# A five-stage transformer kernel on one core: a fixed order of two engines at the stages' ends, and later places for two pieces of the fourth stage

## The chip, the cores and the metric

The kernel runs on one core of a Trainium2 chip. The metric is the device time of one execution in microseconds (us), as the median of several runs. Engines are called as the profile calls them: PE (TensorE, matrix products), DVE (VectorE), ACT (ScalarE), POOL (GpSimd), SP (SyncE, which here only issues DMAs).

## The reference, cut to what matters

Two blocks run one after the other on a sequence of 256 tokens of width 1024. The first is two layers of a hybrid mixer, the second a feed-forward part, an attention and gating part ("mix") and another feed-forward part. Every part normalises its input, multiplies it by large weight matrices and adds the result to the running activations:

```python
def hybrid_layer(x, norm_g, w_in, ..., w_out, rel_bias):
    u = split_columns(rmsnorm(x, norm_g) @ w_in)
    ...
    return x + jnp.concatenate([y_ml, y_gla, y_dsa], axis=-1) @ w_out

def second_block(x, ...):
    h = h + 0.5 * swiglu(rmsnorm_2(h, ffn1_norm[l]), ffn1_w_gate[l], ffn1_w_up[l], ffn1_w_down[l])
    n = rmsnorm_2(h, mix_norm[l])
    z = n @ w_in[l]
    ...
    gm = chunked_spatial_gating(zg[..., :G_WIDTH], zg[..., G_WIDTH:], ...)
    gates = jax.nn.sigmoid(n @ w_gate[l] + b_gate[l])
    merged = gates[..., :D] * (attn @ w_branch_attn[l]) + gates[..., D:] * (gm @ w_branch_gmlp[l])
    h = h + merged @ w_out[l]
    h = h + 0.5 * swiglu(rmsnorm_2(h, ffn2_norm[l]), ffn2_w_gate[l], ffn2_w_up[l], ffn2_w_down[l])
    return rmsnorm_2(h, final_norm)
```

The spatial gating multiplies a lower-triangular 128x128 matrix per channel group (`gmlp_w_s`) with the layer-normalised half of z.

## The kernel before

**Stages.** `run` goes through five stages: layer0, layer1, ffn1, mix, ffn2. The running activations `x` stay on the chip as 2 tiles of 128 tokens (t = 0, 1) by 1024 columns.

**Weights.** All weights come as 362 units of 128x1024 floats. `weights` fetches one: a DMA into `raw` (3 buffers), a copy on ACT that rounds it to `hi` (L113), a subtraction on DVE that leaves the rest in `lo` (L114); 5 pairs of `hi` and `lo` exist, so the pair of a unit is free for the unit five later as soon as PE has used it. Each product is made of three matmuls (`mm3`): high by high, high by low, low by high. Activations are split in the same way by `split` (ACT L139 for the high part, DVE L140 for the low part).

**A stage's end.** `out_proj` adds the stage's product to `x`. Its last four units are computed by token tile: for t = 0 and then t = 1, for each half h of the columns, for each of the last two units. After each (t, h) `residual` adds the PSUM result to `x` on DVE (L320, L322 where it is scaled). Once both halves of a token tile are in `x`, `normed` prepares the next stage's input: two squares with row sums on ACT (L308), their sum `r` on DVE (L310), a power on POOL (L311), two products on DVE that write `xs` (L314). `turn` then transposes `xs` on PE in eight 128x128 pieces (`xT`, L223), and `split` makes the high and low parts of the next stage's input of them. The transposes of tile 0 are issued inside the last product of the old stage (t = 1, h = 1, after the first of the two units), those of tile 1 inside the first projection of the next stage (`proj_a`, after three of its four units for tile 0).

**The order of the work.** Instructions are issued in program order with priorities: `high_priority(self.ahead(LEAD))` moves weight fetches up to 500 places forward, normalisation and splits up to 1000. Where an instruction stands in its engine's queue follows from these priorities in a scheduler. Each engine then runs its queue in order. `order(ins)` adds edges that fix the order of the given instructions on one engine without a semaphore.

**Side jobs.** `start` puts a generator on a list, `tick` advances each by one `yield`; the large projections tick after each unit, so that attention and gating pieces are strewn between them. In mix, `attention` computes logits (`al`, L963), a softmax on DVE and ACT (last step L596), waits three ticks, transposes the probabilities on PE (`apT`, L223) and, after both tiles of a head group, multiplies them with the values (`aO`, L981). `spatial` loads the triangular matrices (`wsT`, L1000, 512 KB), clears their upper halves on POOL in eight instructions (L1002), normalises the two tiles of `vg` on DVE (with two small POOL steps `lnr`, L215 and L216, between), and then issues its matmuls (`sgp`, L1025) in two groups of eight. The projection that runs around them is `gatep`, 16 units of 16 matmuls (L200, L201).

Of the kernel before, what the change touches and what calls it, by code (L numbers as in the profile page):

```python
# [34 lines left out]
class Net:  # L35
    def __init__(self, ctx, tc, a, out, dbg=None):
# [18 lines left out]
        self.jobs, self.ready = [], []  # L55
# [46 lines left out]
    def weights(self):  # L102

        nc = self.nc
        if self.ready:
            return self.ready.pop()
        with self.tc.high_priority(self.ahead(LEAD)):
# [5 lines left out]
            nc.scalar.copy(hi, raw)  # L113
            nc.vector.tensor_sub(lo, raw, hi.bitcast(F32))  # L114
        return hi, lo
# [16 lines left out]
    def order(self, ins):  # L132

        for a, b in zip(ins, ins[1:]):
            self.tc.add_manual_dep(b.ins, a.ins.name, NOSYNC, reason="order")

    def split(self, hi, lo, src):

        self.nc.scalar.copy(hi, src)  # L139
        self.nc.vector.tensor_sub(lo, src, hi.bitcast(F32))  # L140
# [8 lines left out]
    def proj_a(self, x, name, by_token=None):  # L149
# [13 lines left out]
        for t in range(2):  # L163
            for u in range(4):
                self.rows(ps, x, 2 * u, u == 0, u == 3, (t,), ws[u])
                if t == 0 and u == 2:
                    self.turn()
# [109 lines left out]
    def norm(self, g_src):  # L277
# [6 lines left out]
        def fill(t):  # L284
            with self.tc.high_priority(self.ahead(2 * LEAD)):
                halves = self.normed(t, g)

            def turn():
                for b, xs in enumerate(halves):
                    ps = self.transposes([xs[:, P * k:P * (k + 1)] for k in range(4)], "xT")  # L290
                    ks, ts = slice(4 * b, 4 * b + 4), slice(P * t, P * (t + 1))
                    with self.tc.high_priority(self.ahead(2 * LEAD)):
                        self.split(xh[:, ks, ts], xl[:, ks, ts], ps)
# [8 lines left out]
    def normed(self, t, g):  # L302
# [4 lines left out]
        for h in range(2):  # L307
            nc.scalar.activation(xs[h], self.x[:, t, 512 * h:512 * (h + 1)], AF.Square, scale=1.0 / 32, accum_out=ss[:, h:h + 1])  # L308
        r = self.small([P, 1], "r")
        nc.vector.scalar_tensor_tensor(r, ss[:, 0:1], EPS, ss[:, 1:2], ALU.add, ALU.add)  # L310
        nc.gpsimd.tensor_tensor(r, r, self.mhalf[:, 0:1], ALU.pow)  # L311
        for h in range(2):
            sl = slice(512 * h, 512 * (h + 1))
            nc.vector.scalar_tensor_tensor(xs[h], self.x[:, t, sl], r, g[:, sl], ALU.mult, ALU.mult)  # L314
        return xs

    def residual(self, t, half, ps, scale=None):
        sl = self.x[:, t, 512 * half:512 * (half + 1)]
        if scale is None:
            self.nc.vector.tensor_add(sl, ps, sl)  # L320
        else:
            self.nc.vector.scalar_tensor_tensor(sl, ps, scale, sl, ALU.mult, ALU.add)  # L322

    def out_proj(self, y, nk, scale=None, need=0):
# [622 lines left out]
    def attention(self, qk, vs, y):  # L947
# [4 lines left out]
        for hg in range(2):  # L952

            pT = self.work([P, 4, 384], "pT2", 2)
            for t in range(2):
# [11 lines left out]
                yield  # L967
                yield
                yield
# [25 lines left out]
    def spatial(self, v, ug, y):  # L995
# [12 lines left out]
        for t in range(2):  # L1008
# [9 lines left out]
            yield  # L1018
        for u in range(2):
# [15 lines left out]
    def run(self, stages):  # L1035
# [16 lines left out]
        for pool, part in (("hybrid", ("layer0", "layer1")), ("ffn1", ("ffn1",)), ("mix", ("mix",)), ("ffn2", ("ffn2",))):  # L1052
# [158 lines left out]
```

## Time and profile before

| what | value |
|---|---|
| device time, median of 3 runs | 1138.05 us (1137.65 to 1139.64) |
| the profiled execution's own time | 1138.0 us |
| its span | 1136.3 us |
| PE busy | 1119.2 us, 98% of the span |
| DVE, ACT, POOL busy | 813.2 us (72%), 616.6 us (54%), 93.6 us (8%) |
| chain that ended last, by engine | PE 90%, DVE 6%, ACT 2%, DMA 1% |
| granted TensorE clock | 9 tenths or more in all 40 slices |

The span is the time from the first to the last instruction of the program; the device time holds another 1.7 us around it. A busy PE says only that matmuls overlap without a hole in the record: matmuls of 512 columns take 0.39 us each in the record but start every 0.23 us. So lost time is read from the starts of neighbouring matmuls.

### The profile page before, as it was taken

The numbers are of one execution on the slowest core, as the hardware profiler recorded it, in microseconds if no ns is written. First come the engines' busy times: TensorE is split into PE (matmuls) and PEld (weight loads), VectorE is DVE, ScalarE is ACT, GpSimd is POOL, SyncE is SP. The second block draws the span as 40 slices with busy tenths as digits, with TensorE's granted clock in tenths as the row PEclk, the third lists the DMA queues.
The fourth block names the chain that finished last, engine by engine and source line by source line (L and its number), as shares of the span: only waits on it lengthen the run. The fifth ranks groups of instructions, "written<-read, shape, count | busy, mean of one in ns | idle before, by whom it ended". The sixth has DMA issues, their size and how long they took to land.

```text
span 1136.3 us, 16695 instructions
## 1 busy us (share of the span) xinstructions
PE 1119.2 (98%) x6330; PEld 962.0 (85%) x6330; DVE 813.2 (72%) x1236; ACT 616.6 (54%) x950; POOL 93.6 (8%) x133
## 2 busy tenths in 40 slices
PE   8999999999999999999999999999999999999997
PEld 5888889898798888989878888887887997888886
DVE  5697897886668879778756777646597577777743
ACT  5645755554465576456445555434566545555532
POOL 1111101121011210112100000000001000000000
PEclk9999999999999999999999999999999999999999
DMA  8846545556564654456557565666654565666662
GB/s 274 262 146 205 185 136 158 161 170 189 163 200 146 198 167 143 136 155 180 173 159 225 183 189 187 199 190 198 218 168 131 174 190 177 197 189 188 195 192 75
DMA packets 59465, 203.75 MB, mean 179 GB/s; under 512 B 6700, under 2 KB 9652, under 8 KB 59384
## 3 DMA queue, kind: packets, MB, share of 16 engines
q1 hardware_dynamic: 59384, 202.68, 57.2%
q8 instruction: 50, 0.82, 0.3%
q14 instruction: 31, 0.25, 0.1%
HBM read 201.46 MB, written 2.11 MB: 179 GB/s over the span
## 4 chain that ended last, share of the span: by engine, by line
PE 90%; DVE 6%; ACT 2%; DMA 1%; issue 1%; POOL 0%; SPq 0%; DVEq 0%; POOLq 0%; ACTq 0%
PE op L147 19%; PE fg L200 6%; PE fu L200 6%; PE mq L147 4%; PE mk L147 4%; PE mo L147 4%; PE mz L147 4%; PE mv L147 3%; PE fg L201 3%; PE fu L201 3%; DVE lo L114 2%; PE gatep L200 2%; PE brp L147 2%; PE dz L147 2%; PE iq L147 2%; PE dk L147 2%
## 5 line engine op out<-in xcount | busy, mean ns | idle before, releaser
L114 DVE TENSOR_TENSOR lo<-raw,hi 128x1024 fp32r<-128x1024 f32 x362 | 446.6, 1236 | 223.5 <-ACT hi L113 222.2
L113 ACT CAST hi<-raw 128x1024 fp32r<-128x1024 f32 x362 | 378.7, 1048 | 374.6 <-PE op L147 89.2
L200 PE MATMUL fu<-x,hi 128*128 128x512 f32 x288 | 101.0, 395 | 0.0
L200 PE MATMUL fg<-x,hi 128*128 128x512 f32 x288 | 100.9, 394 | 0.0
L201 PE MATMUL fg<-x,lo 128*128 128x256 f32 x288 | 80.1, 278 | 0.0
L201 PE MATMUL fu<-x,lo 128*128 128x256 f32 x288 | 80.0, 278 | 0.0
L147 PE MATMUL op<-hi,hh 128*128 128x512 f32 x176 | 68.7, 390 | 0.0
L147 PE MATMUL op<-lo,hh 128*128 128x512 f32 x176 | 68.6, 390 | 0.0
L147 PE MATMUL op<-hi,hl 128*128 128x512 f32 x176 | 68.6, 390 | 0.0
L200 PEld LDWEIGHTS fg<-x,hi 128*128 128x128 f32 x288 | 54.1, 188 | 12.6
L200 PEld LDWEIGHTS fu<-x,hi 128*128 128x128 f32 x288 | 54.1, 188 | 12.5
L201 PEld LDWEIGHTS fg<-x,lo 128*128 128x128 f32 x288 | 54.2, 188 | 0.1
L201 PEld LDWEIGHTS fu<-x,lo 128*128 128x128 f32 x288 | 54.2, 188 | 0.0
L311 POOL TENSOR_TENSOR r<-r,mhalf 128x1 f32<-128x1 f32 x12 | 6.6, 554 | 541.7 <-DVE r L310 541.7
L147 PE MATMUL op<-hi,yh 128*128 128x512 f32 x128 | 51.2, 400 | 0.0
L147 PE MATMUL op<-lo,yh 128*128 128x512 f32 x128 | 50.0, 391 | 0.0
L147 PE MATMUL op<-hi,yl 128*128 128x512 f32 x128 | 49.9, 390 | 0.0
L147 PE MATMUL mq<-x,hi 128*128 128x256 f32 x256 | 48.2, 289 | 0.0
L147 PE MATMUL mk<-x,hi 128*128 128x256 f32 x256 | 46.8, 285 | 0.0
L200 PE MATMUL gatep<-x,hi 128*128 128x512 f32 x128 | 46.2, 404 | 0.0
L660 DVE SCALAR_TENSOR_TENSOR cacc<-pad,cols,cacc 128x256 f32<-128x256 f32 x96 | 41.0, 479 | 0.0
L147 PE MATMUL mv<-hi,x 128*128 128x512 f32 x128 | 40.8, 400 | 0.0
(360 smaller groups left out, 2588.6 us busy)
## 6 DMA issues: line engine op xcount, KB each, us to landing
raw<-in_w SPq DMA_DIRECT2D x362, 512.0 KB, 3.5
x<-in_x SPq DMA_DIRECT2D x2, 512.0 KB, 5.1
g_bc<-in_norm_g SPq DMA_DIRECT2D x2, 512.0 KB, 4.3
mlg<-in_ml_norm_g SPq DMA_DIRECT2D x2, 512.0 KB, 5.4
skew<-strips SPq DMA_DIRECT2D x4, 256.0 KB, 5.3
pen<-skew SPq DMA_DIRECT2D x8, 128.0 KB, 2.9
mb<-M SPq DMA_DIRECT2D x2, 512.0 KB, 4.3
g_bc<-in_ffn_norm SPq DMA_DIRECT2D x2, 512.0 KB
```

Source lines behind the costliest of these rows:

```text
L113: nc.scalar.copy(hi, raw)
L114: nc.vector.tensor_sub(lo, raw, hi.bitcast(F32))
L147: self.nc.tensor.matmul(out, lhsT=lhsT, rhs=rhs, start=first and i == 0, stop=last and i == 2)
L200: nc.tensor.matmul(ps, lhsT=wh[:, ks], rhs=self.x2[:, k], start=k == 0, stop=False)
L201: nc.tensor.matmul(ps[:, 1, :], lhsT=wl[:, ks], rhs=self.x2[:, k, 0, :], start=False, stop=k == KT - 1)
L311: nc.gpsimd.tensor_tensor(r, r, self.mhalf[:, 0:1], ALU.pow)
L660: nc.vector.scalar_tensor_tensor(acc[:, c, :], pad[:, c, 1 + i:1 + i + S], w(i), acc[:, c, :], ALU.mult, ALU.add)
```

## The change

At every stage's end but the last, `out_proj` now fetches the first four units of the next stage itself (`fetch`, called u0 to u3 below in their order of use) and gives ACT and DVE one fixed order for what belongs to the end: the four units' copies and subtractions, the squares, the products `xs`, the splits, the residuals. The residual of tile 1's first half stands behind the splits of tile 0. The subtraction of the third unit, u2, goes to POOL behind the power of tile 0, but not where the next stage is mix (`self.third`). The unit fetched after the last splits is ordered behind them (`self.pins`). In mix, `attention` waits four ticks before it transposes the probabilities where it waited three, and `spatial` waits two more ticks before its matmuls.

```diff
     def weights(self):
         nc = self.nc
         if self.ready:
-            return self.ready.pop()
+            return self.ready.pop(0)
+        return self.fetch()[0]
...
+    def fetch(self, pool=False):
+        nc = self.nc
         with self.tc.high_priority(self.ahead(LEAD)):
             raw = self.wr.tile([P, 1024], F32, tag="raw", name="raw")
             nc.sync.dma_start(raw, self.a["w"][self.unit])
             self.unit += 1
             hi = self.ws.tile([P, 1024], F32R, tag="hi", name="hi")
             lo = self.ws.tile([P, 1024], F32R, tag="lo", name="lo")
-            nc.scalar.copy(hi, raw)
-            nc.vector.tensor_sub(lo, raw, hi.bitcast(F32))
-        return hi, lo
+            a = nc.scalar.copy(hi, raw)
+            b = (nc.gpsimd if pool else nc.vector).tensor_tensor(lo, raw, hi.bitcast(F32), ALU.subtract)
+        if self.pins:
+            for i, p in zip((a, b), self.pins):
+                self.order([p, i])
+            self.pins = None
+        return (hi, lo), (a, b)
...
                 if t == 0 and u == 2:
-                    self.turn()
+                    self.pins = self.turn()[-1]
...
         ws = [[self.weights() for h in range(2)] for g in range(2)]
+        more = self.next_gain is not None
+        units = [self.fetch()] if more else []
+        act = [units[0][1][0]] if more else []
+        dve = [units[0][1][1]] if more else []
         for t in range(2):
             for h in range(2):
                 for g in range(2):
                     self.rows(ps[h], y, 2 * (n - 2 + g), False, g == 1, (t,), ws[g][h])
-                    if t == 1 and h == 1 and g == 0:
-                        self.turn()
+                    if more and (t, h, g) == (1, 1, 0):
+                        units += [self.fetch(), self.fetch(self.third)]
+                        act += [units[1][1][0], units[2][1][0]]
+                        dve.append(units[1][1][1])
+                        if self.third:
+                            self.order([last, units[2][1][1]])
+                        for a, b in self.turn():
+                            act.append(a)
+                            dve.append(b)
+                        if not self.third:
+                            dve.append(units[2][1][1])
+                        dve.append(early)
                 with self.tc.high_priority(self.ahead(2 * LEAD)):
-                    self.residual(t, h, ps[h][t], scale)
+                    early = self.residual(t, h, ps[h][t], scale)
+                if not more or (t, h) != (1, 0):
+                    dve.append(early)
+            if more and t == 1:
+                units.append(self.fetch())
+                act.append(units[3][1][0])
+                dve.append(units[3][1][1])
             self.turn = done(t)
+            act += self.steps[0]
+            dve += self.steps[1]
+            last = self.steps[2]
+        self.order(act)
+        self.order(dve)
+        self.ready = [u[0] for u in units]
...
                 pr = self.softmax(lg, 4, n)
-                yield
-                yield
-                yield
+                for _ in range(4):
+                    yield
...
             nc.vector.tensor_tensor(v[:, t, :], v[:, t, :], b, ALU.add)
             yield
+        yield
+        yield
         for u in range(2):
             ps = self.bank([P, 2, 2, P], "sgp")
...
+                    self.third = stages[i:i + 1] != ["mix"]
```

`self.steps` holds the two squares, the two products and the power that `normed` issued for a tile.

**The end of the first stage on DVE and ACT.** `op` is the old stage's product, `x_2691` the next stage's split input. DVE before:

```order
L310 SCALAR_TENSOR_TENSOR r<-ss 128x1
L314 SCALAR_TENSOR_TENSOR xs_2991<-x,r,g_bc 128x512
L314 SCALAR_TENSOR_TENSOR xs_2992<-x,r,g_bc 128x512
L320 TENSOR_TENSOR x<-op_2693,x 128x512
L114 TENSOR_TENSOR lo<-raw,hi 128x1024 x2
L140 TENSOR_TENSOR x_2691<-xT,x_2691 128x4x128 x2
L320 TENSOR_TENSOR x<-op_2695,x 128x512
L114 TENSOR_TENSOR lo<-raw,hi 128x1024
```

DVE now:

```order
L320 SCALAR_TENSOR_TENSOR r<-ss 128x1
L325 SCALAR_TENSOR_TENSOR xs_2997<-x,r,g_bc 128x512
L325 SCALAR_TENSOR_TENSOR xs_2998<-x,r,g_bc 128x512
L124 TENSOR_TENSOR lo<-raw,hi 128x1024
L149 TENSOR_TENSOR x_2691<-xT,x_2691 128x4x128 x2
L331 TENSOR_TENSOR x<-op_2693,x 128x512
L331 TENSOR_TENSOR x<-op_2695,x 128x512
L124 TENSOR_TENSOR lo<-raw,hi 128x1024
```

ACT before, then ACT now:

```order
L308 ACTIVATE xs_2992,ss<-x 128x512
L113 CAST hi<-raw 128x1024 x2
L308 ACTIVATE xs_3041,ss<-x 128x512
L113 CAST hi<-raw 128x1024
L139 CAST x_2691<-xT 128x4x128 x2
L308 ACTIVATE xs_3042,ss<-x 128x512
```

```order
L318 ACTIVATE xs_2998,ss<-x 128x512
L123 CAST hi<-raw 128x1024 x2
L148 CAST x_2691<-xT 128x4x128 x2
L123 CAST hi<-raw 128x1024
L318 ACTIVATE xs_3065,ss<-x 128x512
L318 ACTIVATE xs_3066,ss<-x 128x512
```

On DVE one subtraction instead of two, and no residual, stands between the products and the splits of tile 0; the other subtraction has left for POOL. On ACT the splits stand directly behind the two copies.

**POOL and SP around mix.** The rows run from the end of ffn1 through mix (`r` is the power at a stage's end). POOL before, then POOL now:

```order
L311 TENSOR_TENSOR r<-r,mhalf 128x1 x4
L215 TENSOR_SCALAR lnr<-bmv 128x1
L216 TENSOR_TENSOR lnr<-lnr,mhalf 128x1
L215 TENSOR_SCALAR lnr<-bmv 128x1
L216 TENSOR_TENSOR lnr<-lnr,mhalf 128x1
L1002 AFFINE_SELECT wsT<-wsT 128x128 x8
```

```order
L321 TENSOR_TENSOR r<-r,mhalf 128x1
L124 TENSOR_TENSOR lo<-raw,hi 128x1024
L321 TENSOR_TENSOR r<-r,mhalf 128x1 x3
L224 TENSOR_SCALAR lnr<-bmv 128x1
L225 TENSOR_TENSOR lnr<-lnr,mhalf 128x1
L1038 AFFINE_SELECT wsT<-wsT 128x128 x8
L224 TENSOR_SCALAR lnr<-bmv 128x1
L225 TENSOR_TENSOR lnr<-lnr,mhalf 128x1
```

SP before, then SP now:

```order
L109 DMA raw<-in_w 128x1024
L274 DMA b_8164<-in_gmlp_ln_b 128x512
L274 DMA g_bc<-in_ffn_norm 128x1024
L109 DMA raw<-in_w 128x1024 x21
L1000 DMA wsT<-in_gmlp_w_s 128x1024
L109 DMA raw<-in_w 128x1024 x30
```

```order
L119 DMA raw<-in_w 128x1024
L283 DMA b_8120<-in_gmlp_ln_b 128x512
L283 DMA g_bc<-in_ffn_norm 128x1024
L119 DMA raw<-in_w 128x1024 x20
L1036 DMA wsT<-in_gmlp_w_s 128x1024
L119 DMA raw<-in_w 128x1024 x32
```

POOL has the subtraction of u2 behind the first power of a stage's end, and the eight selects stand ahead of the second `lnr`. On SP the load of `wsT` stands two units earlier in the stream (one unit less before these rows, and one less in them): it follows the load for the seventh unit of `gatep` where it followed that for the ninth. On PE, the first group of `sgp` stood two matmuls into the fourth unit of `gatep` and was broken into two and six; now all eight follow the fifth unit, and the second eight the sixth. The last probabilities' transposes of the first head group stood 13 matmuls into the first unit of `gatep`, and stand behind its second unit now.

## Rows read from the trace of the kernel before

**Rows 1.** The page, part 1: busy time, share, instructions.

```profile
PE 1119.2 (98%) x6330; PEld 962.0 (85%) x6330; DVE 813.2 (72%) x1236; ACT 616.6 (54%) x950; POOL 93.6 (8%) x133
```

(The columns of rows 2 to 9: start, duration in us, engine, line, operation, what, count, idle time before.)

**Rows 2.** Timeline of PE, end of the first stage.

```profile
302.03 1.03 PE L223 MATMUL xT<-ident,xs 128*128 128x128 f32 x8
...
304.06 0.40 PE L147 MATMUL op<-lo,yh 128*128 128x512 f32 x1
304.71 0.51 PE L147 MATMUL dq<-hi,x 128*128 128x512 f32 x1 [0.25 <-ACT x L139]
305.44 0.50 PE L147 MATMUL dq<-hi,x 128*128 128x512 f32 x1 [0.22 <-DVE x L140]
...
309.40 1.24 PE L223 MATMUL xT<-ident,xs 128*128 128x128 f32 x8
310.40 0.70 PE L147 MATMUL dq<-hi,x 128*128 128x512 f32 x2
```

**Rows 3.** Timeline of DVE, the same stretch.

```profile
300.47 1.42 DVE L314 SCALAR_TENSOR_TENSOR xs<-x,r,g_bc 128x512 f32<-128x512 f32 x2 [0.68 <-POOL r L311]
...
302.40 2.35 DVE L114 TENSOR_TENSOR lo<-raw,hi 128x1024 fp32r<-128x1024 f32 x2
304.69 1.29 DVE L140 TENSOR_TENSOR x<-xT,x 128x512 fp32r<-128x512 f32 x2
...
306.49 1.22 DVE L114 TENSOR_TENSOR lo<-raw,hi 128x1024 fp32r<-128x1024 f32 x1
307.63 0.15 DVE L310 SCALAR_TENSOR_TENSOR r<-ss 128x1 f32<-128x1 f32 x1
308.45 1.41 DVE L314 SCALAR_TENSOR_TENSOR xs<-x,r,g_bc 128x512 f32<-128x512 f32 x2 [0.67 <-POOL r L311]
```

**Rows 4.** Timeline of ACT, the same stretch.

```profile
299.50 2.23 ACT L113 CAST hi<-raw 128x1024 fp32r<-128x1024 f32 x2
...
304.09 1.06 ACT L139 CAST x<-xT 128x512 fp32r<-128x512 f32 x2
```

**Rows 5.** Timeline of POOL, the same stretch: the power of tile 1.

```profile
307.86 0.56 POOL L311 TENSOR_TENSOR r<-r,mhalf 128x1 f32<-128x1 f32 x1 [7.43 <-DVE r L310]
```

**Rows 6.** Timelines of POOL and DVE in layer 0: both at work at once.

```profile
168.20 3.53 POOL L735 TENSOR_TENSOR srg<-srg,g 128x512 f32<-128x512 f32 x2 [26.02 <-DVE srg L734]
...
168.64 1.91 DVE L114 TENSOR_TENSOR lo<-raw,hi 128x1024 fp32r<-128x1024 f32 x1
...
231.14 2.34 POOL L711 TENSOR_TENSOR sz_z<-sz_z,mlg 128x512 f32<-128x512 f32 x1
...
231.11 1.23 DVE L114 TENSOR_TENSOR lo<-raw,hi 128x1024 fp32r<-128x1024 f32 x1 [0.24 <-ACT hi L113]
```

**Rows 7.** Timelines of ACT and DVE, end of mix: around the second `xs`.

```profile
940.92 1.05 ACT L113 CAST hi<-raw 128x1024 fp32r<-128x1024 f32 x1
...
942.02 0.68 DVE L322 SCALAR_TENSOR_TENSOR x<-op,x 128x512 f32<-128x512 f32 x1
```

**Rows 8.** Timeline of PE in mix: matmuls around the waits.

```profile
842.63 0.39 PE L200 MATMUL gatep<-x,hi 128*128 128x512 f32 x1
843.40 1.06 PE L223 MATMUL apT<-ident,lg 128*128 128x128 f32 x8 [0.37 <-DVE lg L596]
...
852.94 0.28 PE L201 MATMUL gatep<-x,lo 128*128 128x256 f32 x1
854.07 0.43 PE L1025 MATMUL sgp<-wsT,vg 128*64 128x128 f32 x2 [0.84 <-POOL wsT L1002]
855.35 0.43 PE L1025 MATMUL sgp<-wsT,vg 128*64 128x128 f32 x2 [0.85 <-POOL wsT L1002]
```

**Rows 9.** Timelines of SP and POOL in mix.

```profile
847.36 0.33 SPq L109 DMA_DIRECT2D raw<-in_w  x1
847.74 0.42 SPq L1000 DMA_DIRECT2D wsT<-in_gmlp_w_s  x1
...
853.72 4.43 POOL L1002 TENSOR_SCALAR_AFFINE_SELECT wsT<-wsT 128x128 f32<-128x128 f32 x8 [11.86 <-DMA wsT<-in_gmlp_w_s]
```

More of the change, by code (lines that the diff above doesn't have):

```diff
@@ L54, in __init__ @@
         self.unit = 0
-        self.jobs, self.ready = [], []
+        self.jobs, self.ready, self.pins = [], [], None
         self.consts()
@@ L105, in weights, with order @@
         if self.ready:
-            return self.ready.pop()
+            return self.ready.pop(0)
+        return self.fetch()[0]
+    def order(self, ins):
+        for a, b in zip(ins, ins[1:]):
+            self.tc.add_manual_dep(b.ins, a.ins.name, NOSYNC, reason="order")
+    def fetch(self, pool=False):
+        nc = self.nc
         with self.tc.high_priority(self.ahead(LEAD)):
@@ L130, in join @@
             self.tick()
-    def order(self, ins):
-        for a, b in zip(ins, ins[1:]):
-            self.tc.add_manual_dep(b.ins, a.ins.name, NOSYNC, reason="order")
     def split(self, hi, lo, src):
-        self.nc.scalar.copy(hi, src)
-        self.nc.vector.tensor_sub(lo, src, hi.bitcast(F32))
+        a = self.nc.scalar.copy(hi, src)
+        return a, self.nc.vector.tensor_sub(lo, src, hi.bitcast(F32))
     def mm3(self, out, w, x, swap, first, last):
@@ L285, in fill @@
             with self.tc.high_priority(self.ahead(2 * LEAD)):
-                halves = self.normed(t, g)
+                halves, self.steps = self.normed(t, g)
             def turn():
+                splits = []
                 for b, xs in enumerate(halves):
@@ L292, in turn @@
                     with self.tc.high_priority(self.ahead(2 * LEAD)):
-                        self.split(xh[:, ks, ts], xl[:, ks, ts], ps)
+                        splits.append(self.split(xh[:, ks, ts], xl[:, ks, ts], ps))
+                return splits
             return turn
@@ L306, in normed @@
         xs = [self.tmp([P, 512], f"xs{h}") for h in range(2)]
-        for h in range(2):
-            nc.scalar.activation(xs[h], self.x[:, t, 512 * h:512 * (h + 1)], AF.Square, scale=1.0 / 32, accum_out=ss[:, h:h + 1])
+        sq = [nc.scalar.activation(xs[h], self.x[:, t, 512 * h:512 * (h + 1)], AF.Square, scale=1.0 / 32, accum_out=ss[:, h:h + 1]) for h in range(2)]
         r = self.small([P, 1], "r")
         nc.vector.scalar_tensor_tensor(r, ss[:, 0:1], EPS, ss[:, 1:2], ALU.add, ALU.add)
-        nc.gpsimd.tensor_tensor(r, r, self.mhalf[:, 0:1], ALU.pow)
+        pw = nc.gpsimd.tensor_tensor(r, r, self.mhalf[:, 0:1], ALU.pow)
+        st = []
         for h in range(2):
             sl = slice(512 * h, 512 * (h + 1))
-            nc.vector.scalar_tensor_tensor(xs[h], self.x[:, t, sl], r, g[:, sl], ALU.mult, ALU.mult)
-        return xs
+            st.append(nc.vector.scalar_tensor_tensor(xs[h], self.x[:, t, sl], r, g[:, sl], ALU.mult, ALU.mult))
+        return xs, (sq, st, pw)
     def residual(self, t, half, ps, scale=None):
@@ L319, in residual @@
         if scale is None:
-            self.nc.vector.tensor_add(sl, ps, sl)
+            return self.nc.vector.tensor_add(sl, ps, sl)
         else:
-            self.nc.vector.scalar_tensor_tensor(sl, ps, scale, sl, ALU.mult, ALU.add)
+            return self.nc.vector.scalar_tensor_tensor(sl, ps, scale, sl, ALU.mult, ALU.add)
     def out_proj(self, y, nk, scale=None, need=0):
@@ L1076, in write @@
             with self.tc.high_priority(self.ahead(2 * LEAD)):
-                for h, xs in enumerate(self.normed(t, g)):
+                halves, self.steps = self.normed(t, g)
+                for h, xs in enumerate(halves):
                     self.nc.sync.dma_start(self.out[0, P * t:P * (t + 1), 512 * h:512 * (h + 1)], xs)
```

## The prediction

> **What bounds the kernel now.** I read the page first: PE is busy for 1119.2 us of a span of 1136.3 [rows 1], so only time in which PE starts no matmul can be won, and the other engines matter where PE waits for them. A busy record hides short holes, so I then read the starts of matmuls in the timeline of PE, and for each hole the timelines of the engines that end it. Two kinds of holes belong to this change.
>
> At a stage's end the last product matmul starts at 304.06. Matmuls follow each other every 0.23 us there (17 of them from 305.44 to 309.40), so the next stage's first could start at 304.29. It starts at 304.71, for the high part of the input from ACT, and the second at 305.44, for the low part from DVE: 0.42 and 0.50 lost [rows 2]. The reason is in the queues: DVE does a residual and two subtractions (302.40, 2.35 us) before the splits (304.69, 1.29 us) [rows 3], and ACT a square and a copy between its two copies, which end at 299.50 + 2.23 = 301.73, and its split at 304.09 [rows 4]. The transposes started at 302.03 [rows 2], so PE had given the data long before. The other three stage ends with a next stage repeat this.
>
> In mix PE waits three times: for the softmax before the probabilities' transposes (843.40, where the matmul before it, at 842.63, would have let it start 0.23 us later: 0.54 lost), and twice for the triangular matrices (854.07, which could have followed 852.94, a matmul of 256 columns, by half of 0.23: 1.01 lost; and again before 855.35, 0.85 us idle and some 0.2 for the restart) [rows 8]. Their load is issued at 847.74, right behind a weight load, and the selects on POOL begin at 853.72 and take 4.43 us [rows 9].
>
> **A stage's end after the change.** I follow the first one, from the second `xs`, which ends at 300.47 + 1.42 = 301.89 [rows 3]. An instruction that follows on DVE starts 0.08 us before its predecessor ends (306.49 + 1.22 against 307.63) [rows 3].
>
> - DVE subtracts u1 from 301.81 to 303.02 (1.21 us, half of the pair). ACT is free since 301.73 and splits the first four transposes as soon as they are there, about 302.7, so its two halves end at 303.25 and 303.75. DVE's splits then run from 303.28 to 304.57. PE finds the high part at 304.29 and the first low half (303.97) at 304.52. Both holes close: 0.92 us.
> - For tile 1, two residuals (0.68 each [rows 7]) reach to 305.77, u3's subtraction (1.22) to 306.9, `r` (0.15) to 306.97, the power on POOL (0.56, begun 0.08 after `r`, as 307.63 + 0.15 against 307.86 [rows 3, 5]) to 307.61, the products (1.41) to 309.06. ACT has copied u3 (1.05) by 304.7 and squares each half as its residual ends, so it is in time. Before, PE went on after tile 1's transposes at 310.40, which is 0.54 after the products ended (308.45 + 1.41 = 309.86) [rows 2, 3]. So now it goes on at 309.60: **0.8 us** won. Late next are these products: PE reaches the transposes at 304.29 + 18 x 0.233 = 308.5 and waits about 0.3 for their second half.
> - At the end of ffn1, u2 stays on DVE, between splits and residuals: the products end 1.14 later. But there PE does four matmuls more (0.93) before the transposes; 0.8 - 1.14 + 0.93 = **0.6 us**.
>
> **The subtraction on POOL** (three ends) has no row in this kernel. Nearest is a product of two SBUF inputs of 512 columns: in layer 0 one starts at 231.14, waits for the DVE subtraction that had started at 231.11 and ends at 232.34, and ends at 233.48: 1.14 us of its own, so 2.28 for 1024 columns, if it scales [rows 6]. From 303.02 that gives 305.3, and PE needs u2 at 304.29 + 12 x 0.23 = 307.1. The splits and residuals, which read PSUM, go on beside it. So its price is nothing, as long as the next stage's third unit covers it; the lower bound of its price is nothing too, the upper one is rival 1.
>
> That it starts after u1's subtraction is my choice, and a narrow one. The same rows show the other order: POOL's product began at 168.20, DVE's subtraction at 168.64 took 1.91 us instead of 1.22 [rows 6]. Whoever starts first holds the other up. Here DVE would start u1 at 301.81, and POOL u2 0.08 after its copy ends at 301.73: also 301.81. At the end of mix the copy ends at 941.97, so POOL would start at 942.05, and DVE's next instruction starts at 942.02 [rows 7]. I take DVE as first, because it leads by 0.03 there and 0.03 decided at 231.11 [rows 6].
>
> The Trainium skill (SBUF — State Buffer, Who interferes with whom) says that a DVE instruction with two SBUF inputs and a POOL instruction that reads SBUF take one shared port, for the whole instruction, by order of issue. Rows 6 agree, in both orders; by that rule the sum is this one with DVE first and rival 1's with POOL first.
>
> **Mix.** `apT` of the first group moves 19 matmuls later on PE while its logits move 16 later, and the softmax is reordered by about as much, so its 0.54 has three matmuls' time to close. The load of `wsT` is issued two units earlier in the stream, and the matmuls that need it come nearly two units later (after five units of `gatep` instead of three and two matmuls). A unit is 16 matmuls, half of them of 512 and half of 256 columns, an estimate of 8 x (0.23 + 0.12) = 2.8 us. Today the selects end at 858.15 [rows 9] while PE wanted them from 853.06; 5.1 us late against a shift of 5.6 + 5.2 = 10.8: 1.01 and 1.05 go. That makes **2.6 us** (between 2.06, the idle time alone [rows 8], and 2.8 if smaller restarts go too; nothing, if the cover is gone).
>
> What is queued behind the new order: DVE's normalisation of `vg`'s second tile waits for a `lnr` that now stands behind the selects on POOL, up to 4.43 us [rows 9], and weight subtractions wait behind it. I cost this at nothing, since a subtraction there is done two to three units (5 to 8 us) before PE uses it. SP's reordered small loads cost nothing for the same reason: three raw buffers lie ahead. DVE's three saved subtractions (3.7 us) are worth nothing by themselves, PE being the bound. The units ordered behind the last splits are ready some 4 us before PE reaches them.
>
> **Sum.** 3 x 0.8 + 0.6 + 2.6 = 5.6 us off the profiled execution's own 1138.0 (span 1136.3 and 1.7 around it), which is 0.05 below the median: **1132.4 us**.
>
> **Rivals.**
>
> 1. *POOL takes the port first at all three ends.* It holds it from 301.89 for 2.28; u1's subtraction ends at about 305.25 instead of 303.02. The splits end at 306.5 (the second matmul waits until 305.9, half a microsecond longer than today), and the chain of tile 1 ends at 310.96, so PE goes on at 311.5 instead of 310.40: 1.1 lost at each end. For: the tie above. Against: the 0.03. -3 x 1.1 + 0.6 + 2.6 is about 0: **1138.1**, no change.
> 2. *POOL takes it at some.* Each end lost costs 0.8 + 1.1 = 1.9: one **1134.3**, two **1136.2**.
> 3. *Mix keeps its waits*, because DVE hangs behind the selects or the softmax is as late as before; the change then does half of what it says. For: nearly every DVE and ACT instruction of that stretch stands in a new place. Against: 10.8 us of shift against 5.1. 5.6 - 2.6 = 3.0 won: **1135.0**.
> 4. *Slower: POOL first at all three, and the subtraction on POOL is slow.* The two products at 168.20 took 3.53 us together [rows 6], 1.77 each with their waiting; at that rate 1024 columns hold the port for 3.5. Each end then loses 1.1 + 1.2 = 2.3, three 6.9, against 3.2 won: **1141.7**. It is slower by 0.2% from a hold of about 3.0 us on. Against: the plain rate is 1.14 per 512.
>
> **How the numbers follow.** 0.2% is 2.3 us, about what a measurement of this kernel can tell from no change; faster means under 1135.8. Forecast 0.60; rival 1 0.13; one end lost 0.09 and two 0.05; rival 3 0.07; rival 4 0.06. Faster: 0.60 + 0.09 + 0.07 = 0.76. Same: 0.13 + 0.05 = 0.18. Slower: 0.06. Rivals 1 and 4 (0.19) are left out of the range. Its top takes in two lost ends (1136.2) and the scatter of runs, 1137.0; its bottom lets every stage end run without the last 0.3 (1.2 in all) and mix give 2.8: 1130.8.
>
> **What would show it.** Right: the first matmul of a new stage starts 0.23 after the last `op`; the subtraction on POOL starts with u1's on DVE, which stays at 1.2 us, and ends some 3.5 us later; PE's list of waits loses `sgp` and `apT`; the selects end before the fifth unit of `gatep`. Wrong: u1's subtraction lasts over 3 us (rival 1, 2), a POOL subtraction alone over 3 us (rival 4), or PE still waits for POOL or DVE inside mix (rival 3).

## The result, and the profile after

The change takes 1132.32 us (median, 1131.14 to 1133.36); the kernel before takes 1138.57 in the same comparison. The ratio is 0.9949, 95% interval [0.9935, 0.9964]: faster, 0.1 us from the forecast. In a later comparison it was 1133.19 against 1137.5, ratio 0.9965 [0.9953, 0.9977]. The profiled execution of the change took 1133.35 us of its own, with this page:

```profile
span 1131.6 us, 16690 instructions
...
PE 1118.4 (99%) x6330; PEld 962.3 (85%) x6330; DVE 810.8 (72%) x1233; ACT 616.3 (54%) x950; POOL 105.0 (9%) x136
...
PEclk8999999999999999999999999999999999999999
...
PE 95%; DVE 3%; ACT 1%; DMA 1%; issue 0%; SPq 0%; POOL 0%; DVEq 0%; POOLq 0%; ACTq 0%
```

DVE falls by 2.4 us and POOL rises by 11.4, of which three subtractions of 3.5 us (with their waiting) are 10.4 [rows 1]. The chain goes over PE for 95% where it was 90%: fewer waits for DVE.

**A stage's end.** The timeline of PE after, end of the first stage (all times are 1.49 us later than before: the second `xs` ran at 301.96 where it was 300.47 [rows 3]):

```profile
305.56 0.39 PE L156 MATMUL op<-lo,yh 128*128 128x512 f32 x1
305.79 0.62 PE L156 MATMUL dq<-hi,x 128*128 128x512 f32 x2
...
310.03 1.29 PE L232 MATMUL xT<-ident,xs 128*128 128x128 f32 x8
311.08 0.71 PE L156 MATMUL dq<-hi,x 128*128 128x512 f32 x2
```

The first matmul of the new stage follows the last `op` by 0.23, without a wait; before, it followed by 0.65, and two waits stood there [rows 2]. PE goes on behind tile 1's transposes at 311.08, 5.52 after the last `op`; before, it was 6.34. DVE in the same stretch:

```profile
303.29 1.22 DVE L124 TENSOR_TENSOR lo<-raw,hi 128x1024 fp32r<-128x1024 f32 x1
304.77 1.29 DVE L149 TENSOR_TENSOR x<-xT,x 128x512 fp32r<-128x512 f32 x2 [0.26 <-ACT x L148]
305.98 1.28 DVE L331 TENSOR_TENSOR x<-op,x 128x512 f32<-128x512 f32 x2
307.18 1.22 DVE L124 TENSOR_TENSOR lo<-raw,hi 128x1024 fp32r<-128x1024 f32 x1
...
309.13 1.42 DVE L325 SCALAR_TENSOR_TENSOR xs<-x,r,g_bc 128x512 f32<-128x512 f32 x2 [0.67 <-POOL r L321]
```

POOL in the same stretch:

```profile
303.31 3.48 POOL L124 TENSOR_TENSOR lo<-raw,hi 128x1024 fp32r<-128x1024 f32 x1 [1.38 <-ACT hi L123]
```

The near tie of the prediction came out DVE first at all three ends with POOL, where its record starts 0.02 to 0.03 us ahead: at the second one and at the end of mix the timeline of POOL has

```profile
592.77 3.48 POOL L124 TENSOR_TENSOR lo<-raw,hi 128x1024 fp32r<-128x1024 f32 x1 [1.38 <-ACT hi L123]
...
938.11 3.46 POOL L124 TENSOR_TENSOR lo<-raw,hi 128x1024 fp32r<-128x1024 f32 x1 [1.40 <-ACT hi L123]
```

and that of DVE

```profile
592.75 1.22 DVE L124 TENSOR_TENSOR lo<-raw,hi 128x1024 fp32r<-128x1024 f32 x1
...
938.08 1.22 DVE L124 TENSOR_TENSOR lo<-raw,hi 128x1024 fp32r<-128x1024 f32 x1
```

DVE keeps its 1.22 us each time, and POOL's 3.48 is that plus 2.28 of its own. The tie is less narrow than these rows suggest. Nine of the traces have the two subtractions within 0.1 us of each other, at 29 ends in all, and DVE comes first at every one. That holds too at the two ends where POOL's record starts first, by 0.04 (37 and 38 ns). One of them is the end of ffn1 in the kernel with POOL at all ends (below), on POOL and on DVE:

```profile
774.50 3.53 POOL L124 TENSOR_TENSOR lo<-raw,hi 128x1024 fp32r<-128x1024 f32 x1 [1.33 <-ACT hi L123]
...
774.53 1.22 DVE L124 TENSOR_TENSOR lo<-raw,hi 128x1024 fp32r<-128x1024 f32 x1
```

So with starts this close, the recorded start does not tell which engine gets through first; what does was not tried.

**The end of ffn1** is the weak one. The timeline of PE there:

```profile
785.33 1.32 PE L232 MATMUL xT<-ident,xs 128*128 128x128 f32 x8 [0.22 <-DVE xs L325]
786.40 0.47 PE L156 MATMUL v2p<-hi,x 128*128 128x512 f32 x1
...
786.94 0.95 PE L156 MATMUL v2p<-hi,x 128*128 128x512 f32 x2
```

It waits for `xs`, and the pair of matmuls at 786.94 takes 0.95 where such a pair takes 0.62: the second one, the fourth matmul behind the transposes, waits for tile 1's low half.

**Mix.** The timeline of PE in the change:

```profile
845.63 0.28 PE L210 MATMUL gatep<-x,lo 128*128 128x256 f32 x1
845.75 1.03 PE L232 MATMUL apT<-ident,lg 128*128 128x128 f32 x8
...
857.22 0.28 PE L210 MATMUL gatep<-x,lo 128*128 128x256 f32 x1
857.43 1.09 PE L1063 MATMUL sgp<-wsT,vg 128*64 128x128 f32 x16
```

That of POOL:

```profile
845.95 4.20 POOL L1038 TENSOR_SCALAR_AFFINE_SELECT wsT<-wsT 128x128 f32<-128x128 f32 x8 [11.65 <-PE gatep L210]
850.13 0.18 POOL L224 TENSOR_SCALAR lnr<-bmv 128x1 f32<-128x1 f32 x1
```

That of SP, the load of `wsT`:

```profile
841.22 0.42 SPq L1036 DMA_DIRECT2D wsT<-in_gmlp_w_s  x1
```

The selects end at 850.15, 7 us before PE needs them, where they ended 5.1 too late [rows 8, 9]; the waits for `wsT` and for the softmax are gone.

**Where the time went, by stretch.** PE does the same work in all kernels here, so I compare when the same matmul starts in two traces. A stretch runs from the first matmul of one part to the first of the next; the stretches of an end reach from the first `op` matmul to 42 matmuls of the next stage. Ends 1 to 4 are those of layer0, layer1, ffn1 and mix. The table gives, in us, what each took more (+) or less (-) than before; the medians of the runs stand beside it, each with that of the kernel before in the same comparison.

| kernel | end 1 | end 2 | ffn1 | end 3 | mix | end 4 | ffn2 | last end | median, before |
|---|---|---|---|---|---|---|---|---|---|
| the change | -0.80 | -0.78 | 0.00 | -0.31 | -3.55 | -0.79 | 0.00 | -0.01 | 1132.32, 1138.57 |
| the change again | -0.79 | -0.79 | 0.00 | -0.32 | -3.55 | -0.80 | +1.76 | -0.01 | 1133.19, 1137.5 |
| ends only | -0.83 | -0.81 | 0.00 | -0.32 | -1.69 | -0.78 | 0.00 | +0.02 | 1135.52, 1137.1 |
| mix only | +0.01 | +0.02 | 0.00 | -0.01 | -3.55 | +0.01 | +0.01 | 0.00 | 1134.22, 1137.1 |
| spatial ticks alone | +0.02 | +0.01 | 0.00 | -0.01 | -2.74 | +0.01 | 0.00 | 0.00 | 1134.75, 1137.5 |
| no POOL | -0.25 | -0.26 | 0.00 | -0.31 | -3.55 | -0.25 | 0.00 | 0.00 | 1133.18, 1137.1 |
| residual ahead of u1 | +0.51 | +0.50 | 0.00 | -0.32 | -3.76 | +0.53 | +0.01 | -0.02 | 1137.11, 1137.57 |
| residual first | -1.16 | -1.13 | 0.00 | -0.27 | -3.55 | -1.16 | +1.76 | -0.02 | 1132.14, 1137.57 |
| the same, POOL at all ends | -1.15 | -1.13 | 0.00 | -1.17 | -3.55 | -1.16 | +1.76 | -0.01 | 1131.46, 1137.57 |
| the same, first at three | -1.17 | -1.17 | 0.00 | -1.17 | -3.76 | -0.79 | 0.00 | 0.00 | 1131.17, 1137.5 |
| small write ahead of u1 | +0.16 | +0.22 | +1.76 | +1.37 | -4.00 | -0.20 | 0.00 | +1.75 | 1138.59, 1137.1 |
| one tile more | +0.15 | +0.17 | +1.76 | +1.36 | -4.39 | -0.20 | 0.00 | +1.74 | 1139.85, 1137.57 |
| stage 64 bytes on | +0.15 | +0.18 | 0.00 | +1.37 | -4.14 | -0.21 | 0.00 | +1.72 | 1136.62, 1137.5 |

Layer 1 stays within 0.1 everywhere, and layer 0 moves from -0.88 to +0.37 with no pattern. The edits won 6.2 in the profiled execution of the change, but its span is only 4.7 shorter: layer 0 gave 0.9, and 2.3 were lost in the first 22 us, where the granted clock was low. The window of 10 to 22 us, before (the last three numbers are the granted clock, the DMA share and GB/s):

```profile
10.00:22.00 12.00, 10.65 (x43) 8.44 (x44) 8.65 (x13) 6.13 (x9) 1.02 (x2) 0.86 0.90 296
```

and after

```profile
10.00:22.00 12.00, 9.85 (x33) 7.42 (x34) 8.66 (x14) 5.83 (x8) 1.24 (x2) 0.72 0.93 292
```

The mean of 0.72 means that a part of it went at the lower level (1.2 of 2.4 GHz), after 10 us in which PE had done 16 matmuls; 33 fitted in where before had 43. In the change, matmuls of 512 columns still started every 0.43 us from 15.3 to 19.1. Before had a shorter part at that level (0.86) and lost nothing by it against the runs at 1.00: by 15.0 its matmuls started every 0.23 us, and up to 14.5 or later PE waits for the low half of its first weights in the runs at 1.00 too. The first 22 us of all other runs agree with those of before within 0.25 us, so this is no part of the change.

### The profile page after: what moved, and what is told of

Its sections match the earlier page's. It is cut to its first block, busy times and chain, and to the rows that moved or that the text cites. A ratio compares the mean times of both kernels' runs of the same rounds, so it can differ in the third digit from the quotient of the medians.

```text
span 1131.6 us, 16690 instructions
## 1 busy us (share of the span) xinstructions
PE 1118.4 (99%) x6330; PEld 962.3 (85%) x6330; DVE 810.8 (72%) x1233; ACT 616.3 (54%) x950; POOL 105.0 (9%) x136
## 4 chain that ended last, share of the span: by engine, by line
PE 95%; DVE 3%; ACT 1%; DMA 1%; issue 0%; SPq 0%; POOL 0%; DVEq 0%; POOLq 0%; ACTq 0%
PE op L156 20%; PE fg L209 6%; PE fu L209 6%; PE mq L156 4%; PE mk L156 4%; PE mo L156 4%; PE mz L156 4%; PE mv L156 4%; PE fg L210 3%; PE fu L210 3%; PE gatep L209 3%; PE dq L156 2%; PE dz L156 2%; PE brp L156 2%; PE iq L156 2%; PE dk L156 2%
```

## The experiments

**Each part alone.** The first kernel is the change without the two edits in mix. The second is the kernel before with these two edits and nothing else. The diff is that of the first:

```diff
-                for _ in range(4):
+                for _ in range(3):
                     yield
...
             yield
-        yield
-        yield
         for u in range(2):
             ps = self.bank([P, 2, 2, P], "sgp")
```

> The fixed order at the stages' ends alone (mix ticks as before). Parts theory: the ends give 0.8 at three and 0.3 at the one before mix, 2.7 us in all, so 2.7 below before; in mix PE waits again for the softmax (about 0.5) and the triangular matrices (about 2). Rival (the ends' gain comes back later as waits in mix): within 1 us of before.

> The later places in mix alone (stage ends as before). Parts theory: the stretch of mix gives its 3.5 us by itself, so 3.5 below before, and the two experiments add up to the change. Rival (mix gains only because DVE is relieved of subtractions and units come earlier at the ends): under 1 us.

Measured: 1135.52 (ratio 0.9986 [0.9975, 0.9997]) and 1134.22 (0.9973 [0.9963, 0.9983]). In the profiled executions the ends give the same four gains alone, and the mix edits the same 3.55. What I had not expected is that mix gains 1.69 with the ends alone. POOL in that kernel's mix:

```profile
850.28 4.59 POOL L1038 TENSOR_SCALAR_AFFINE_SELECT wsT<-wsT 128x128 f32<-128x128 f32 x8 [10.99 <-PE gatep L210]
```

and PE:

```profile
840.82 1.06 PE L232 MATMUL apT<-ident,lg 128*128 128x128 f32 x8 [0.62 <-DVE lg L633]
...
850.62 0.89 PE L1061 MATMUL sgp<-wsT,vg 128*64 128x128 f32 x4
```

The load of `wsT` is issued at 845.18 there, 5.1 us before the selects where it was 5.98 [rows 9], so they begin before PE asks. The second stop is nearly gone as well, for a reason that the prediction did not have. Before, the second select stood beside a subtraction on DVE, and PE's second wait ended with it; the quickest selects take 0.29. POOL, then DVE, before:

```profile
853.97 1.32 POOL L1002 TENSOR_SCALAR_AFFINE_SELECT wsT<-wsT 128x128 f32<-128x128 f32 x1
...
853.92 1.23 DVE L114 TENSOR_TENSOR lo<-raw,hi 128x1024 fp32r<-128x1024 f32 x1
```

With the ends alone it falls beside shorter work:

```profile
850.53 0.49 POOL L1038 TENSOR_SCALAR_AFFINE_SELECT wsT<-wsT 128x128 f32<-128x128 f32 x1
```

The wait for the softmax grows from 0.37 to 0.62. So the parts do not add: by stretches the gains are 4.4, 3.6 and 6.2. That is read from one execution of each kernel. By the medians the ends alone win 1.6 and the mix edits 2.9, and the ten runs of the ends alone lie up to 5.5 apart, so their gain in mix may not be in every run. The mix edits make these waits safe, where the ends alone leave them to when a load lands.

**The spatial matmuls alone**, in the kernel before:

```diff
             yield
+        yield
+        yield
         for u in range(2):
             ps = self.bank([P, 2, 2, P], "sgp")
```

> The kernel before with one edit of the change: the spatial matmuls two ticks later; the softmax's transposes and the stage ends stay. It splits the 3.54 us that mix gained against the 2.6 forecast. Theory (two waits with their restarts, independent of each other): the waits at the spatial matmuls go with their restarts, 2.2 to 2.4 us, and the wait at the probabilities' transposes (0.5, with a restart of some 0.2) stays: mix stretch -2.3, so about 1135.7. Rival (the transposes gain from the spatial matmuls' move): -3.0 or more, or the transposes' wait grows and less than 2 is left.

Measured: -2.74 in mix, between the two expectations. PE in mix:

```profile
842.74 1.06 PE L223 MATMUL apT<-ident,lg 128*128 128x128 f32 x8 [0.37 <-DVE lg L596]
...
856.70 0.63 PE L223 MATMUL apT<-ident,lg 128*128 128x128 f32 x4 [0.20 <-ACT gpre L204]
...
859.49 1.09 PE L1027 MATMUL sgp<-wsT,vg 128*64 128x128 f32 x16
```

The wait for the softmax stays as it was [rows 8], and the change wins 0.81 beyond this. Not all of that is the softmax's tick: four later transposes wait for ACT here, at 856.70, as they do neither before nor in the change. They start 0.59 behind the matmul before them (856.11) and not 0.23, so 0.36 is lost there and some 0.45 is left for the tick (an estimate).

**What POOL brings.** The change with u2's subtraction left on DVE at all ends:

```diff
-                        units += [self.fetch(), self.fetch(self.third)]
+                        units += [self.fetch(), self.fetch()]
...
-                    self.third = stages[i:i + 1] != ["mix"]
+                    self.third = False
```

> As the change, but u2's subtraction stays on DVE at all four ends (behind the splits, as before mix). Order theory: each of the three ends gives 0.3 to 0.6 instead of 0.8, because the products of tile 1 end 1.1 later and the transposes stand four matmuls later: 0.6 to 1.5 us above the change. Rival (the relief of DVE is the gain): the three ends give nothing, 2.4 above the change.

Measured: each of the three ends wins 0.25 in place of 0.79, a little under the 0.3 to 0.6 expected. So by stretches the fixed order alone is worth 0.25, and the subtraction on POOL 0.54 an end. The medians do not show it: 1133.18, and 1133.19 for the change in its later comparison, whose profile has 1.76 of another cause against it (ffn2, below).

**POOL first.** First attempt, a small write on DVE ahead of u1's subtraction:

```diff
+        nc = self.nc
...
+                        if self.third:
+                            z = self.small([P, 1], "late")
+                            dve.append(nc.vector.memset(z, 0.0))
                         dve.append(units[1][1][1])
```

> As the change, with one memset of 128x1 on DVE between the second product and u1's subtraction, at the three ends where POOL has u2. Port theory: POOL's subtraction now starts first by some 0.05 us and holds u1's up: u1's lasts 3.4 to 3.5 us instead of 1.2, POOL's 2.4 instead of 3.5; each of the three ends loses 1.9 us against the change, 5.7 in all, about the time of before. Rival (the engines share the port, or the order does not matter): the time of the change, at most 0.3 above.

A miss: DVE still took the port first. Its timeline at the first end:

```profile
302.40 1.22 DVE L124 TENSOR_TENSOR lo<-raw,hi 128x1024 fp32r<-128x1024 f32 x1
302.43 0.06 DVE L364 MEMSET late<- 128x1 f32 x1
```

and POOL's:

```profile
302.48 3.42 POOL L124 TENSOR_TENSOR lo<-raw,hi 128x1024 fp32r<-128x1024 f32 x1 [1.45 <-ACT hi L123]
```

The write stands first in DVE's queue but is recorded 0.03 behind the subtraction's start, so it held nothing back. The run tells nothing on the port, and lost time elsewhere (below). The second attempt adds no instruction; tile 1's first residual, which reads PSUM, goes ahead of u1's subtraction. Its counterpart (the second diff) has these two the other way round, and at all four ends:

```diff
+                        if self.third:
+                            dve.append(early)
                         dve.append(units[1][1][1])
...
                         if not self.third:
                             dve.append(units[2][1][1])
-                        dve.append(early)
+                            dve.append(early)
```

```diff
+                        dve.append(early)
                         for a, b in self.turn():
...
-                        dve.append(early)
```

> The change with one instruction in another place: at the three ends with POOL, tile 1's first residual stands ahead of u1's subtraction on DVE and not behind the splits. DVE's list is as long as in the change, but its subtraction begins 0.6 us after POOL's. Theory (who issues first holds the shared port for its whole instruction): POOL's subtraction takes about 2.3 us, DVE's subtraction of u1 begins 0.6 us behind it and lasts 2.9 us where it lasted 1.22, the splits come 1.9 us later than with the same residual behind them, PE waits over a microsecond for tile 0's second low half and goes on after tile 1's transposes about 1.3 us later than in the change: some 4 us over the three ends, so about 1136.2, against 1132.3. Rival (the near tie did not matter; the two share without loss): u1's subtraction keeps 1.22 us, the splits come 0.6 us later than in the change, and the ends stay within 0.3 us of it: 1132 to 1133.

> The change with tile 1's first residual behind u1's subtraction and ahead of the splits, at all four ends: the counterpart of the run before, the same list with u1's subtraction and that residual exchanged. Theory: DVE still begins its subtraction first, which keeps 1.22 us; the splits come 0.6 us later (tile 0's first low half at about the time at which PE wants it, a wait of 0.1 to 0.5), the chain of tile 1 is as long as before, since the same DVE work stands ahead of the second residual. ACT's square of the first half begins over a microsecond earlier, which only counts if ACT ends that chain. So 0 to 0.5 us per end worse than the change: 1132.3 to 1134.3. Rival (the chain of tile 1 waits for ACT's squares): up to 0.3 us per end better, 1131.3.

Measured: 1137.11 (ratio 0.999 [0.9979, 1.0]) and 1132.14 (0.9956 [0.994, 0.9973]). POOL at the first end, with that residual ahead of u1's subtraction:

```profile
301.26 2.39 POOL L124 TENSOR_TENSOR lo<-raw,hi 128x1024 fp32r<-128x1024 f32 x1 [1.38 <-ACT hi L123]
```

DVE there:

```profile
301.25 0.68 DVE L331 TENSOR_TENSOR x<-op,x 128x512 f32<-128x512 f32 x1
301.85 2.89 DVE L124 TENSOR_TENSOR lo<-raw,hi 128x1024 fp32r<-128x1024 f32 x1
304.66 1.28 DVE L149 TENSOR_TENSOR x<-xT,x 128x512 fp32r<-128x512 f32 x2
```

PE there:

```profile
303.74 0.39 PE L156 MATMUL dq<-hi,x 128*128 128x512 f32 x1
305.40 0.50 PE L156 MATMUL dq<-hi,x 128*128 128x512 f32 x1 [1.27 <-DVE x L149]
```

POOL's subtraction takes 2.39 when it is first, and DVE's, begun 0.59 behind it, 2.89: it ends 1.09 after POOL's, near its own 1.22, as if it had started then. Each end loses 1.3 us against the change, 3.9 in three, as expected from the lock. The residual, begun with POOL and reading PSUM, keeps its 0.68. With u1 ahead, the same list wins 0.36 an end on the change. DVE in that kernel (POOL's subtraction takes 3.49 there):

```profile
301.40 1.22 DVE L124 TENSOR_TENSOR lo<-raw,hi 128x1024 fp32r<-128x1024 f32 x1
302.54 0.69 DVE L331 TENSOR_TENSOR x<-op,x 128x512 f32<-128x512 f32 x1
303.14 1.28 DVE L149 TENSOR_TENSOR x<-xT,x 128x512 fp32r<-128x512 f32 x2
```

The gain has the size of that run's rival, but not its reason: in the change DVE idles before the splits, for ACT (they start 1.48 after u1's subtraction, which lasts 1.22); here it does a residual in that time, and from u1's subtraction to `r` the chain of tile 1 is 0.36 shorter (4.66 for 5.02). ACT's squares do not end it: `r` starts without a wait in both. I had counted the same work ahead of the second residual, and not the idle time in it.

**POOL at the end of ffn1 too**, on top of the counterpart:

```diff
-                    self.third = stages[i:i + 1] != ["mix"]
+                    self.third = True
```

> As the kernel with tile 1's first residual ahead of the splits, and the third unit's subtraction on POOL at the end of ffn1 too, where DVE did it; PE's order there becomes that of the other ends. Theory: DVE is freed of 1.2 us ahead of the residuals at that end, so the three waits of PE there (0.38, 0.17 and 0.21 us in the change) go down to those of the other ends; the end of ffn1 gains 0.8 on the kernel before in place of 0.3: 0.5 us better than its neighbour in this set. Rival: POOL is still busy with work for the next stage (its third unit waits behind it), and that end loses up to 1 us.

Measured: 1131.46, ratio 0.9942 [0.9927, 0.9957]. That end wins 1.17 in place of 0.27, more than the 0.5 expected, and its waits are nearly gone, as PE shows there:

```profile
781.05 1.17 PE L232 MATMUL xT<-ident,xs 128*128 128x128 f32 x8
781.97 0.70 PE L156 MATMUL v2p<-hi,x 128*128 128x512 f32 x2
```

**Two paces of the same matmuls.** The small write and the counterpart both lost 1.8 us or more in stretches that they do not touch. Three kernels look for the reason: one small tile more and nothing else; 64 bytes of padding more; and the order of the change at the end of mix alone:

```diff
+        if self.third and not hasattr(self, "late"):
+            self.late = self.small([P, 1], "late")
+            self.nc.gpsimd.memset(self.late, 0.0)
```

```diff
-        self.gap(pool("tail"), 384)
+        self.gap(pool("tail"), 448)
```

```diff
+                        if self.soon:
+                            dve.append(early)
                         for a, b in self.turn():
...
-                        dve.append(early)
+                        if not self.soon:
+                            dve.append(early)
...
+                    self.third = True
+                    self.soon = s != "mix"
```

> The change with one more small tile (one column, two buffers) that is written once and never read; the order at the stage ends is the change's. It asks why the kernel with a small write ahead of u1's subtraction lost 1.8 us over ffn1's products, 1.4 at its end product and 1.8 over the last stretch, in matmuls that the edit did not touch and at a granted clock of 1.00. Theory (the addresses of what is allocated behind the small tile): the same three stretches lose the same amounts here, about 5 us: 1137. Rival (the extra instruction, or the places that it moved): they stay within 0.1 us of the change: 1132.3.

> The change with 64 bytes more of padding ahead of the stage's buffers, so that these (the outputs of the layers and the ffn's hidden halves, which PE reads in the end products, among them) lie 64 bytes further on; no instruction is added and no order changed. In the kernels with one small tile more every end product ran at one matmul of 512 columns per 233.3 ns where the change has 226.7, at the same granted clock. Theory (the address of what PE reads there): all five end products run at 233.3 here as well, about 0.9, 0.9, 1.4, 0.4 and 1.7 us: 1137.5, or 1139.3 if ffn1's products slow down too. Rival (the tile's extra instruction, or chance): they stay at 226.7 and the time at 1132.3.

> POOL takes the third unit at all four ends, and tile 1's first residual stands ahead of the splits at three of them; at the end of mix the order is the change's. With that residual ahead at all four, each end gained 0.35 on the change, but ffn2's products ran slower by 1.76 us throughout (matmuls of 512 columns next to ones of 256 at 236 ns in place of 232, at the same granted clock). Theory (how PE enters the stage sets the rhythm of its products): with the change's order at the end of mix ffn2 runs as in the change, and the time is that of the kernel with all four ends less 1.76 and more 0.35: 1130.0. Rival (the rhythm has another cause): ffn2 stays slow, 1131.8.

> The change as it is, beside the last kernel on one chip. The record of its first profile began at a granted clock of 0.83 and lost 2.3 us in the first 22 us; all later ones began at 1.00. Theory: the start is no part of the change, its profile is shorter by 2.3 here, 1131.1, with all stretches as in the first, and the median lies between 1131.1 and 1133.4. Rival: the change itself starts slower, and the profile shows it again.

Measured: 1139.85 (1.0013 [0.9999, 1.0026]), 1136.62 (0.9994 [0.9984, 1.0003]), 1131.17 (0.9946 [0.9932, 0.9961]) and 1133.19. Windows of the end product of ffn1 (730 to 770) and of ffn2's products (985 to 1045), with PE's busy time and its number of matmuls first; in the first profile of the change:

```profile
730.00:770.00 40.00, 40.00 (x179) 33.10 (x177) 17.91 (x15) 15.82 (x15) 0.00 (x0) 1.00 0.62 190
985.00:1045.00 60.00, 60.00 (x348) 52.47 (x347) 44.56 (x60) 33.82 (x54) 0.00 (x0) 1.00 0.62 190
```

with 64 bytes of padding:

```profile
730.00:770.00 40.00, 40.00 (x173) 32.06 (x172) 17.15 (x14) 15.37 (x15) 0.00 (x0) 1.00 0.61 185
```

in the change again:

```profile
985.00:1045.00 60.00, 60.00 (x342) 52.05 (x341) 43.61 (x60) 33.09 (x53) 0.00 (x0) 1.00 0.60 185
```

The granted clock is 1.00 in all of them, and PE has no idle time. Two things are told apart. The padding slows the end product from 179 matmuls in 40 us to 173, and all five end products lose 0.6 to 1.8 us against the change, in the three kernels whose stage buffers lie 64 bytes on (the small tile moves them as far) and in none of the others: the address is shown to be the reason, by an edit that adds no instruction. The shift is not slow everywhere. In the same three kernels, and in no other, the 192 matmuls of the branch products in mix (`brp`) take 22.50 us where they take 22.91, so 0.4 of what they win in mix is this. (Mix wins 0.2 to 0.8 more than the change in five kernels; the rest of that was not followed.) Why the address matters was not tried. ffn2's products have another cause. The kernel with the change's order at the end of mix ran them at the faster pace, as its theory said, but the change itself ran them at 348 in its first profile and at 342 in its second. So the theory that the order at the end of mix sets their pace falls, and the 1.76 us that the counterpart lost there need not be a price of its order. The second profile of the change also has the start of before (within 0.12), as expected, but not the expected length: this pace took 1.76 back. What sets that pace in one execution, and ffn1's in the two kernels with the tile, stays open.

## Why the prediction was right, point by point

- **The three ends with POOL** (3 x 0.8): 0.80, 0.78, 0.79. The chain holds step by step: on the first end's clock the splits started at 303.28 and PE went on at 309.59, against 303.28 and 309.60.
- **POOL at no price.** DVE was first at all three, and POOL's own 2.28 is the estimate from layer 0 [rows 6]. The choice was right, but not its reason: a lead of 0.03 in the records was taken to decide, and at two ends DVE is first with POOL's record 0.04 ahead. The lock is now shown in this kernel by both orders (1.22 and 2.89). The Trainium skill (SBUF — State Buffer, Who interferes with whom) gives the same rule, an exclusive lock that goes by order of issue, and the trace agrees. Rival 1 was priced at 1.1 lost per end; the kernel in which POOL is first lost 0.5, and as it has the residual ahead, which alone wins 0.36, some 0.9 is the like figure (an estimate).
- **The end of ffn1** (0.6): 0.31. The step "the products end 1.14 later, PE does four matmuls more" holds up to the transposes: PE went on 6.67 after the last `op`, 1.15 more than at the first end. What failed is that I stopped there: the low half of tile 1 is later too. With four matmuls done ahead, PE asks for it as the fourth behind the transposes and not as the eighth, and waits the missing 0.3. The three ends of the kernel without POOL's subtractions have the same order of PE and come out alike (0.25).
- **Mix** (2.6): 3.55. The mechanism was right, and the rivals with it in doubt are out: no wait for POOL or DVE is left, and the second `lnr`, which starts right behind the selects at 850.13, held nothing up that PE waited for. The size was short in one term. The spatial matmuls alone gave 2.74, and some 3.1 without the new wait of that run, where I had 2.06; the transposes are left with some 0.45 where I had 0.54. I priced the waits of `sgp` and hardly its pieces: before, it began with four matmuls in two pieces, which kept PE for 2.77 (from 852.94 to 855.71), went on with twelve, for 0.81, and was cut by `apT`. It runs in two unbroken groups now. Nor was the late load the whole cause of its second wait, as the slow select above shows.
- **The sum** is 6.2 by stretches where the forecast was 5.6, and 6.25 by the medians (4.3 in the later comparison, where the profile of the change has 1.76 of ffn2's pace against it). That the forecast came within 0.1 is partly luck: two errors of size (0.3 too much and 0.95 too little) made the gain 0.65 larger, and the kernel before was 0.57 slower in the comparison than the 1138.0 that the forecast started from. The scatter of the start and of ffn2's pace, each about 2 us, lies around it. The bottom of the range is added up wrongly: 3.0, 1.2 and 2.8 off 1138.0 make 1131.0 and not 1130.8; nothing hangs on it.

## What to carry to other kernels

Follow the chain past the point where the bound engine resumes to the next thing that it asks for, and price a wait with the restarts around it. Where two engines can hold each other up, place in front of the second one an instruction that the first does not hold up, so that the order does not hang on a near tie: the residual in front of u1's subtraction put POOL 0.59 ahead, and that decided. A queue that idles for another engine just before the critical step can do there what it must do anyway: with the residual there at three ends, and POOL's subtraction at all four, the kernel took 1131.17 against 1133.19 for the change in the same comparison (1.6 in the ends, by stretches).

## What the runs showed of the hardware

- A matmul stream with no idle time and a granted clock of 1.00 has two paces, some 3% apart in the end products (179 and 173 in 40 us) and 1.7% in ffn2 (348 and 342 in 60 us). In the first a shift of the stage's buffers by 64 bytes decides, and the same shift makes another product (`brp`) 1.8% faster; in the second the pace differs between two executions of one kernel. The runs of one kernel differ by 0.5 to 5.5 us; such a pace (1.76 a stage) and the start are of that size.
- The granted clock in the first 22 us varied between executions of the same instructions (0.72 to 1.00 in 10 to 22 us), and the lowest cost 2.3 us.
- A subtraction of two SBUF inputs on DVE and one on POOL go one after the other: 1.22 and 3.48 us with DVE first, 2.39 and 2.89 with POOL 0.59 ahead. With recorded starts within 0.1 us of each other DVE was first at all 29 ends, also with POOL's record 0.04 ahead. A select on POOL (128x128) begun at or just behind the start of such a subtraction took 1.3 to 1.7 us (three traces of mix), others 0.29 to 0.77.
